# Moving the end of one row of x to the end of the queue, with new cuts of the last loads

## The chip, the cores and the metric

One core of one Trainium2 chip. The metric is the device time of one execution in microseconds; a program on one core has one such time per execution. All runs quoted here are of the fast state and had a granted clock of 1.0.

## The reference

```python
batch, dim = 1024, 4096            # x and y: float32, random normal
def reference(x, y, axis):          # axis = -1
    return np.sum((x - y) ** 2, axis=axis).astype(np.float32)
```

Each of the 128 partitions gets 8 rows of 4096 columns, so 32,768 columns of x and as many of y. "Columns" below are columns per partition: 128 columns of one input are 128 x 128 x 4 bytes, 65.5 KB.

## The kernel before

All loads are issued from one engine (SyncE) and so form one queue. Lists of widths say how x and y are cut. VectorE subtracts (into x's buffer), ACT squares and sums; the last piece alone is squared and summed by VectorE, in one fused instruction that starts from ACT's partial sum of row 3. The parts that the argument touches:

```python
xw = [4096, 12288, 8192, 5472, 1280, 960, 320, 160]
yw = [16256, 8192, 2624, 2784, 1344, 480, 480, 288]
late, last = 128, 192
LATE = 3
halved = (1, 2, 3, 4)                 # loads of y whose pieces are cut in two
cut = (LATE + 1) * D - late           # the last 128 columns of row 3 ...
# [...] xs is xw in order; ys is yw in order without those 128 columns, and then
ys += [(N - last, N), (cut, cut + late)]   # ... come last of all of y
# [...]
    order = []                        # an x load goes ahead of the first y load that needs it
    have = 0
    for c0, c1 in ys:
        while have < c1:
            order.append((landed_x, xv, X, "x") + xs[len([o for o in order if o[3] == "x"])])
            have = order[-1][5]
        order.append((landed_y, yv, Y, "y", c0, c1))
# [...]
    for j, (c0, c1) in enumerate(ys):
        final = j == len(ys) - 1
        wait_loaded(c1, landed_y[j][1])           # VectorE waits for y and the x it needs
        for piece in pieces_of(j, c0, c1):
            sub(*piece)                           # VectorE: x - y
            if final:                             # VectorE: square, sum, add ACT's sum
                nc.vector.wait_ge(diffs, n["diffs"])
                nc.vector.tensor_tensor_reduce(...)
                continue
            square(*piece, where[piece])          # ACT: square with a sum
# [...]
        if j == 4:
            for r in (4, 5, 6):
                complete(r)           # VectorE adds the parts of a row
    complete(7)                       # waits for ACT's last sum
    nc.sync.wait_ge(sums, n["sums"])
    nc.sync.dma_start(out=ov, in_=results).then_inc(stored, 16)
```

## Time and profile before

| | before |
|---|---|
| time, median of the first 3 runs | 83.98 us (83.97 to 84.12) |
| span of the profiled execution | 82.6 us |
| DMA engines, share of the span | 95.9% |
| VectorE, ACT | 45%, 40% |
| last load landed / last reduction starts / store issued | 80.25 / 80.99 / 81.18 us |

The prediction below shows the page's lines, the waits, the chain of waits and the end of the timeline. One reading of the trace recurs here: the landing records. A load's semaphore is incremented 16 times, once for each DMA engine that carries a part of it, and a wait for the load is satisfied at the sixteenth. This is as the Trainium skill has it ("DMA: Bandwidth & Descriptors", section "Why a DMA increments its semaphore by 16 and not by 1"); the trace has 16 records for each of the 18 loads and for the store. In the kernel before, the sixteen increments of a load lay 0.21 to 0.26 us apart from first to last. "Landed" is the last of them, "mean landing" the mean of the sixteen.

### The profile page before, as it was taken

How to read it: one execution, taken by the hardware profiler on the slowest of the kernel's cores; microseconds unless marked ns; L12 is line 12 of the kernel's file. 1: busy time of each engine (PE TensorE's matmuls, PEld its weight loads, DVE VectorE, ACT ScalarE, POOL GpSimd, SP SyncE). 2: the span in 40 equal slices, each digit the busy share in tenths (PEclk: the TensorE clock that was granted, in tenths of full speed). 3: DMA queues.
4: the chain of work that ended last, by engine and by line, in shares of the span. 5: the costliest groups of instructions: out<-in, count | busy, mean ns of one | idle time of the engine just before them, and what ended most of it. 6: DMA issues, size and time to landing. Idle time of an engine off the chain costs nothing.

```text
span 82.6 us, 136 instructions
## 1 busy us (share of the span) xinstructions
DVE 36.8 (45%) x27; ACT 33.4 (40%) x41; POOL 0.2 (0%) x4
## 2 busy tenths in 40 slices
DVE  0000000000000000000299999999189996989992
ACT  3300000000000000000000979889896999899991
POOL 0000000000000000000000000000000000000000
DMA  5998998888999991999599699969979799999960
GB/s 127 389 500 381 595 547 381 381 381 381 504 504 504 504 504 63 441 504 504 254 508 508 286 476 508 476 286 508 423 339 509 339 437 440 426 402 416 395 220 2
DMA packets 2736, 33.56 MB, mean 406 GB/s; under 512 B 432, under 2 KB 1328, under 8 KB 1712
## 3 DMA queue, kind: packets, MB, share of 16 engines
q1 hardware_dynamic: 2736, 33.56, 95.9%
HBM read 33.55 MB, written 0.00 MB: 406 GB/s over the span
## 4 chain that ended last, share of the span: by engine, by line
DMA 63%; SPq 16%; DVE 12%; ACT 4%; issue 1%
DMA Y<-in_y_dram 63%; SPq L108 16%; DVE X L175 11%; ACT X L181 4%; DVE Y L204 0%; DVE results L188 0%; SPq L220 0%; DVE results L204 0%
## 5 line engine op out<-in xcount | busy, mean ns | idle before, releaser
L175 DVE TENSOR_TENSOR X<-X,Y 128x2048 f32<-128x2048 f32 (+10 forms) x21 | 36.2, 1780 | 44.3 <-DMA Y<-in_y_dram 44.3
L181 ACT ACTIVATE X<-X 128x2048 f32<-128x2048 f32 (+9 forms) x20 | 31.2, 1559 | 46.1 <-DVE X L175 46.0
L181 ACT ACTIVATION_READ_ACCUMULATOR X<-X 128x1 f32 x20 | 3.7, 186 | 0.0
L181 ACT ACT_TABLE_LOAD x1 | 1.3, 1283 | 1.4 <-PEq L19 1.4
L188 DVE TENSOR_REDUCE results<-parts 128x1 f32<-128x2 f32 (+2 forms) x4 | 0.4, 152 | 0.0
L204 DVE CUSTOM_DVE_ANT_0 Y<-X,parts 128x128 f32<-128x128 f32 x1 | 0.4, 352 | 0.0
L250 POOL MEMSET const-bfloat16-1.0<- 128x1 bf16 x1 | 0.1, 101 | 0.0
L250 POOL MEMSET const-uint8-127<- 128x1 uint8 x1 | 0.1, 101 | 0.0
L250 POOL MEMSET const-float32-0.0<- 128x1 f32 x1 | 0.1, 98 | 0.2 <-issue 0.2
L250 POOL MEMSET const-float32-1.0<- 128x1 f32 x1 | 0.1, 98 | 0.0
L204 DVE DVE_READ_ACCUMULATOR2_ANT results<- 128x1 f32 x1 | 0.1, 83 | 0.0
## 6 DMA issues: line engine op xcount, KB each, us to landing
Y<-in_y_dram SPq DMA_DIRECT2D x1, 8128.0 KB, 39.0
X<-in_x_dram SPq DMA_DIRECT2D x1, 6144.0 KB, 20.2
X<-in_x_dram SPq DMA_DIRECT2D x1, 4096.0 KB, 48.3
Y<-in_y_dram SPq DMA_DIRECT2D x1, 4096.0 KB, 57.5
X<-in_x_dram SPq DMA_DIRECT2D x1, 2736.0 KB, 13.3
X<-in_x_dram SPq DMA_DIRECT2D x1, 2048.0 KB, 7.1
Y<-in_y_dram SPq DMA_DIRECT2D x1, 1392.0 KB, 19.0
Y<-in_y_dram SPq DMA_DIRECT2D x1, 1312.0 KB, 16.1
```

The source lines that it names most:

```text
L108: nc.sync.dma_start(out=dst[:, home(c0, c1)], in_=src[:, c0:c1]).then_inc(sem, 16)
L175: nc.vector.tensor_sub(out=a, in0=a, in1=Y[:, home(c0, c1)]).then_inc(diffs, 1)
L181: nc.scalar.activation(out=a, in_=a, func=Square, accum_out=acc).then_inc(acts, 1)
L188: nc.vector.tensor_reduce(out=results[:, r : r + 1], in_=parts_of(r, len(row_parts[r])), axis=mybir.AxisListType.X, op=add,).then_inc(sums, 1)
L204: nc.vector.tensor_tensor_reduce(out=Y[:, home(*piece)], in0=X[:, home(*piece)], in1=X[:, home(*piece)], scale=1.0, scalar=parts_of(r, 1), ...
L250: nc = _bacc.Bacc("TRN2", target_bir_lowering=False, num_devices=1)
```

## The change

The intent: the last 128 columns of row 3 come last of x as well as of y. They add a small load between the last columns of row 7 and the last load of y, so that ACT's last sum and VectorE's fused sum are ready together; the other cuts are fitted to this. The core of the diff (what is left out, the code that waits for the late load of x among it, is marked `[...]`):

```diff
-    xw = [4096, 12288, 8192, 5472, 1280, 960, 320, 160]
-    yw = [16256, 8192, 2624, 2784, 1344, 480, 480, 288]
-    late, last = 128, 192
+    xw = [4096, 12160, 8192, 6784, 736, 384, 288]
+    yw = [16256, 8192, 1344, 1376, 1376, 1376, 1280, 768, 384, 288]
+    late = 128
-    halved = (1, 2, 3, 4)
+    halved = (1, 2, 3, 4, 5, 6, 7)
[...]
-    ys += [(N - last, N), (cut, cut + late)]
[...]
+        return spans + [(cut, cut + late)]
+
+    xs, ys = pieces(xw), pieces(yw)
[...]
-        if j == 4:
+        if j == 6:
             for r in (4, 5, 6):
                 complete(r)
```

The queue ends with (x and y with their columns) x320, y288, x160, y192, y128 before, and x384, y384, x288, y288, x128, y128 after.

More of the change, by code (lines that the diff above doesn't have):

```diff
@@ L68, with pieces @@
     results = nc.alloc_sbuf_tensor("results", [P, R], F32).ap()
-    xw = [4096, 12288, 8192, 5472, 1280, 960, 320, 160]
-    yw = [16256, 8192, 2624, 2784, 1344, 480, 480, 288]
-    late, last = 128, 192
+    xw = [4096, 12160, 8192, 6784, 736, 384, 288]
+    yw = [16256, 8192, 1344, 1376, 1376, 1376, 1280, 768, 384, 288]
+    late = 128
     LATE = 3
-    halved = (1, 2, 3, 4)
+    halved = (1, 2, 3, 4, 5, 6, 7)
     cut = (LATE + 1) * D - late
-    assert sum(xw) == N and sum(yw) == N - late - last
-    xs, c = [], 0
-    for w in xw:
-        xs.append((c, c + w))
-        c += w
-    ys, c = [], 0
-    for w in yw:
-        ys.append((c, c + w))
-        c += w
-        if c == cut:
-            c += late
-    ys += [(N - last, N), (cut, cut + late)]
+    def pieces(widths):
+        spans, c = [], 0
+        for w in widths:
+            spans.append((c, c + w))
+            c += w
+            if c == cut:
+                c += late
+        assert c == N
+        return spans + [(cut, cut + late)]
+    xs, ys = pieces(xw), pieces(yw)
     prog = Program(nc, tc)
@@ L111 @@
     order = []
-    have = 0
-    for c0, c1 in ys:
-        while have < c1:
-            order.append((landed_x, xv, X, "x") + xs[len([o for o in order if o[3] == "x"])])
-            have = order[-1][5]
-        order.append((landed_y, yv, Y, "y", c0, c1))
+    xk = 0
+    for piece in ys:
+        while xk < len(xs) and (xs[xk][0] < piece[1] if xk < len(xs) - 1 else piece == ys[-1]):
+            order.append((landed_x, xv, X, "x") + xs[xk])
+            xk += 1
+        order.append((landed_y, yv, Y, "y") + piece)
     todo = list(order)
@@ L161, with wait_loaded @@
     seen_x = [0]
-    def wait_loaded(c1, ysem):
+    def wait_loaded(c1, ysem, final):
         waits = []
-        while seen_x[0] < len(xs) and xs[seen_x[0]][0] < c1:
+        while seen_x[0] < len(xs) - 1 and xs[seen_x[0]][0] < c1:
             waits.append(seen_x[0])
             seen_x[0] += 1
+        if final:
+            assert seen_x[0] == len(xs) - 1
+            waits.append(seen_x[0])
         nc.vector.wait_ge(ysem, 16)
@@ L197 @@
         final = j == len(ys) - 1
-        wait_loaded(c1, landed_y[j][1])
+        wait_loaded(c1, landed_y[j][1], final)
         for piece in pieces_of(j, c0, c1):
```

## The prediction

> **What bounds the kernel now.** I read the page first: the span, the engines' busy time and the DMA queue.
>
> ```profile
> span 82.6 us, 136 instructions
> ...
> DVE 36.8 (45%) x27; ACT 33.4 (40%) x41; POOL 0.2 (0%) x4
> ...
> q1 hardware_dynamic: 2736, 33.56, 95.9%
> ...
> DMA 63%; SPq 16%; DVE 12%; ACT 4%; issue 1%
> ```
>
> Both compute engines work less than half of the span; the DMA engines work 95.9% of it, which is 79.2 us of 82.6. They carry 33.56 MB, which is exactly both inputs, and the change carries the same bytes. So whatever the change does, it can touch only what is left: the small cost of each load, and what comes after the last byte. Next I read who waited for whom.
>
> ```profile
> DVE X L175 <- DMA Y<-in_y_dram: 44.3, 5, 40.9
> ```
>
> VectorE waited five times, always for a load of y. The first wait (40.9 us, for the 8 MB load) isn't a loss, since loads run under it. What counts is the end, so I read the timeline of the last three microseconds; columns are start, duration, engine, line, operation.
>
> ```profile
> 79.38 0.19 ACT L181 ACTIVATION_READ_ACCUMULATOR X<-X 128x1 f32 x1
> 79.47 0.59 ACT L181 ACTIVATE X<-X 128x480 f32<-128x480 f32 x1
> 79.58 1.06 DVE L175 TENSOR_TENSOR X<-X,Y 128x288 f32<-128x288 f32 x3 [0.15 <-DMA Y<-in_y_dram]
> 79.97 0.19 ACT L181 ACTIVATION_READ_ACCUMULATOR X<-X 128x1 f32 x1
> 80.08 0.44 ACT L181 ACTIVATE X<-X 128x288 f32<-128x288 f32 x1
> 80.42 0.19 ACT L181 ACTIVATION_READ_ACCUMULATOR X<-X 128x1 f32 x1
> 80.52 0.35 ACT L181 ACTIVATE X<-X 128x192 f32<-128x192 f32 x1
> 80.67 0.35 DVE L204 CUSTOM_DVE_ANT_0 Y<-X,parts 128x128 f32<-128x128 f32 x1
> 80.77 0.19 ACT L181 ACTIVATION_READ_ACCUMULATOR X<-X 128x1 f32 x1
> 80.95 0.08 DVE L204 DVE_READ_ACCUMULATOR2_ANT results<- 128x1 f32 x1
> 80.99 0.16 DVE L188 TENSOR_REDUCE results<-parts 128x1 f32<-128x8 f32 x1
> 81.18 0.35 SPq L232 DMA_DIRECT2D out_dram<-results  x1
> ```
>
> The row at 79.58 merges three subtractions: 288, 192 and 128 columns. The last reduction, at 80.99, needs two things: ACT's sum of the 192 columns, read out by 80.96, and VectorE's own fused sum, whose read-out starts at 80.95. So the two arrive together already. After it comes the store: issued at 81.18, landed 1.4 us later at 82.6.
>
> Which load holds this end? The chain of waits stops at this piece:
>
> ```profile
> 66.94 13.12 DMA Y<-in_y_dram
> 80.05 0.02 issue
> 80.08 0.57 DVE X L175 x2
> 80.65 0.03 issue
> 80.67 0.35 DVE Y L204
> ```
>
> So the end is held by the 192-column load of y, landed at 80.05, and not by the last one: the trace's landing records put the 128 columns at 80.25, when VectorE is still in the 192-column subtraction (80.08 to 80.43). The last load is hidden by about 0.1 us.
>
> The same landing records give the price of a load. Landings, with the step from the one before: x5472 66.76; y2624 69.92 (3.16); y2784 73.25 (3.33); x1280 74.78 (1.53); y1344 76.38 (1.60); x960 77.54 (1.16); y480 78.15 and 78.75 (0.60 each); x320 79.15 (0.40); y288 79.56 (0.41); x160 79.79 (0.23); y192 80.05 (0.26); y128 80.25 (0.20). The 8192-column y took 9.72 us for 4.19 MB, 432 GB/s. At that rate 128 columns (65.5 KB) are 0.15 us and took 0.20; 480 (246 KB) are 0.57 and took 0.60. One load more therefore costs 0.03 to 0.05 us; I use 0.035.
>
> **What the Trainium skill says.** "ScalarE: Activation LUTs", section "What ACT_TABLE_LOAD costs": an ACTIVATE with immediate scale and bias takes 186 ns plus 0.833 ns per element, and back-to-back ones overlap by some 93 ns. For 288 columns that is 426 ns; the trace has 443, and a step of 0.44 between starts, because the accumulator read-out follows each one. The trace agrees.
> "VectorE: DVE Perf Modes", "Specifications" and "Walkthrough": 0.96 GHz, and fp32 tensor-tensor work has one result per cycle. That is 1.04 ns per column; the trace's 128x4096 (4421 ns) and 128x128 (285 ns) give 1.042 and a fixed 0.15. It agrees.
> "DMA: Bandwidth & Descriptors", "Bandwidth", measures a 64 KB transfer at 0.95 us and calls everything under 64 KB dominated by descriptors (another issue path than this kernel's). This trace doesn't show such a price for a 64 KB load in a full queue: 0.20 us. The measurement decides.
>
> **The change part by part.**
> 1. Loads: 18 become 19. The end of row 3 of x (128 columns) leaves the second load of x and comes next to last. Cost: one load, +0.035 us on the last landing, so 80.25 becomes about 80.29. This lies on the path.
> 2. The second x load is 65.5 KB less, so y16256 lands at 40.69 in place of 40.84 and the next two groups 0.15 us earlier. All of it is off the path: VectorE catches up with the loads again at 69.95 in any case.
> 3. y2624 and y2784 become 1344 and three of 1376. VectorE needs 2 x (672 to 704 x 1.042 ns + about 0.07) = 1.57 us per 1376 columns; the load takes 1.63 + 0.035 = 1.67. ACT needs 2 x (688 x 0.833 ns + 0.19) = 1.53. Both keep up; nothing gained, as both keep up today.
> 4. The last 192-column piece goes. Pieces of row 7 end 768 (two of 384), 384, 288. VectorE's subtractions rise from 21 to 23 and ACT's squares from 20 to 22, two fixed costs of about 0.07 and 0.1 us each per engine, beside loads.
>
> The end, by counting back 0.20 us per 128 columns and 0.37 for 288 from 80.29: x128 80.09, y288 79.89, x288 79.51, y384 79.14, x384 78.65, y768 78.16.
> - VectorE: 384 at 79.16, free by 79.63; 288 at 79.91 to 80.36, next start possible at 80.28; the last 128 at 80.31 to 80.60, just after its landing; fused sum at 80.63 (80.67 now).
> - ACT: 384 columns cost 0.52 per step. Pieces ready at 78.78, 79.25 and 79.75; it is free again by about 80.32. The 288 are ready at 80.40: 0.34 to the read-out, 0.19 for it, done at 80.93 (80.96 now).
> - Reduction at about 80.94 (80.99 now), store issued at 81.13, landed at 82.55.
> Sum: +0.04 for the load, -0.09 for no longer queueing a 192-column subtraction ahead of the last one: **-0.05 us**. From 83.98 that makes 83.93; the ACT side gives -0.03 and VectorE's -0.04, the same within what I can read, and I put down 83.92.
>
> **The rivals.**
> - *The extra small loads cost more than their bytes.* If the page's price for 64 KB held in this queue, the 128-column x would cost up to 0.75 us more: 84.7. Against it: the 128- and 192-column loads of y are there already and took 0.20 and 0.26.
> - *ACT becomes the last.* Its last piece grows from 192 to 288 columns (347 to 443 ns). If ACT is behind by one piece of 384, its end moves from 80.93 to about 81.1: 84.05. For it: at the end now ACT runs piece on piece with no idle. Against: 384-column pieces arrive every 0.47 to 0.5 us and cost 0.52, so only about 0.1 us piles up before the gap ahead of the 288.
> - *The queue runs dry.* The issuing engine stands still for up to 5.57 us at its last issue, so the ring holds some ten loads. With 19 loads the last issue is later still; if smaller loads filled the ring with less work, transfers could stop. Then it would be 84.5 or more. Against: the last issue now ends at 73.0, 7 us ahead of its landing; ten of the new loads hold as much.
> - *A larger gain.* If the old end were held by the 192-column subtraction alone and the extra load were free, it would be the 0.09 plus the 0.035: 83.86. Nothing shows more: after the last byte the subtraction, fused sum, reduction and store all stay.
>
> **Range and chances.** The three runs of before spread over 0.15 us, and the page's terms can each be off by 0.05. The gain and this spread are alike in size, so 83.70 to 84.15 should hold it 8 times in 10. Two per cent is 1.68 us; the rivals make at most +0.7, and to gain 1.68 the DMA engines would have to carry the same bytes faster. Faster by over 2%: 0.01; within 2%: 0.98; slower: 0.01.
>
> **What would show each step right or wrong.** In the changed kernel's landing records: the last y at 80.25 to 80.35 (step 1), with 0.15 to 0.25 us for each 128-column load. In the chain of waits: the last piece must be the 128-column y load and not the one before it. In the timeline: the fused sum at about 80.63, ACT's last read-out ending at about 80.93, the reduction at 80.94. In the waits: more waits of VectorE for loads of y (every group), in about the same total less 0.15. The prediction would be wrong if the last landing moved by more than 0.1 us, if DMA showed slices with idle engines between 60 and 80 us, or if ACT's last read-out ended after 81.05.

## The result, and the profile after

| | before | changed |
|---|---|---|
| median, 6 runs each | 84.06 us (83.97 to 84.12) | 84.12 us (84.08 to 84.43) |
| ratio of fast runs | | 1.0016, 95% interval 0.9999 to 1.0033 |
| loads | 18 | 19 |
| span of the profiled execution | 82.6 us | 82.8 us |

A ratio is the mean time of the one kernel's fast runs over that of the other's of the same rounds, so it is not quite the ratio of the medians: the means are 84.19 and 84.05 us. The class "same" is right. The predicted gain of 0.05 us is not there. The mean of 84.19 lies above the predicted range, which ended at 84.15; the median of 84.12 lies just inside it. All outputs are right.

The page of the changed kernel, lines that answer to those shown of before (engines with busy time, share and instructions; the DMA queue with packets, MB and share; the chain by engine):

```profile
span 82.8 us, 143 instructions
...
DVE 37.1 (45%) x29; ACT 33.9 (41%) x45; POOL 0.2 (0%) x4
...
q1 hardware_dynamic: 2880, 33.56, 96.0%
...
DMA 58%; SPq 22%; DVE 12%; ACT 4%; issue 1%
```

144 packets more (2736 before): the 128 rows of the new load and its 16 semaphore packets. The bytes are the same. The end of the timeline of the changed kernel (start, duration, engine, line, operation):

```profile
79.90 0.51 ACT L185 ACTIVATE X<-X 128x384 f32<-128x384 f32 x1
80.05 0.72 DVE L179 TENSOR_TENSOR X<-X,Y 128x288 f32<-128x288 f32 x2 [0.28 <-DMA Y<-in_y_dram]
80.31 0.18 ACT L185 ACTIVATION_READ_ACCUMULATOR X<-X 128x1 f32 x1
80.54 0.44 ACT L185 ACTIVATE X<-X 128x288 f32<-128x288 f32 x1
80.81 0.35 DVE L208 CUSTOM_DVE_ANT_0 Y<-X,parts 128x128 f32<-128x128 f32 x1
80.89 0.19 ACT L185 ACTIVATION_READ_ACCUMULATOR X<-X 128x1 f32 x1
81.08 0.08 DVE L208 DVE_READ_ACCUMULATOR2_ANT results<- 128x1 f32 x1
81.11 0.16 DVE L192 TENSOR_REDUCE results<-parts 128x1 f32<-128x8 f32 x1
81.30 0.35 SPq L236 DMA_DIRECT2D out_dram<-results  x1
```

and of its chain of waits (start, duration, what):

```profile
71.49 8.96 DMA Y<-in_y_dram
80.46 0.02 issue
80.48 0.30 DVE X L179
80.78 0.03 issue
80.81 0.35 DVE Y L208
```

The form of the end is the predicted one. The chain now ends in the last load itself, VectorE is free when it lands, ACT's read-out (80.89 + 0.19) and VectorE's (from 81.08) arrive together. Read to the nanosecond, the last reduction starts 32 ns after ACT's read-out ends and 28 ns after VectorE's begins; in the kernel before it was 31 and 38. In two of the experiments (before_xlate, xlate_in_2) ACT was done 0.16 and 0.09 us ahead, and the reduction started in the same nanosecond as VectorE's read-out. So in both kernels it is ACT's sum that comes last, by a hair. But all of it stands 0.15 to 0.18 us later than predicted, because the last load landed at 80.456 and not at 80.29. The landing records divide the 0.205 us between the last landings of the two profiles:

| from before to changed, mean landings | us |
|---|---|
| first load (x4096), whose size did not change: 7.015 to 7.060 | +0.045 |
| 128 columns fewer ahead of the 8192 columns of y | -0.15 |
| from that y (60.164, now 60.058) to the last y (80.145, now 80.292): 19.98 to 20.23 | +0.25 |
| slowest engine behind the mean at the last load: 0.106 to 0.164 | +0.06 |
| sum | +0.205 |

The second row takes back 0.15 of the third, for the 128 columns only changed their place. What is left of the third is +0.10 us, in place of the predicted +0.035 for one load. The first and the last row are a matter of the single execution, if they do not come again. The experiments test this.

### The profile page after: what moved, and what is told of

Same layout as the page of the kernel before. It is cut to its first block, busy times and chain, and to the rows that moved or that the text cites. A ratio compares the mean times of both kernels' runs of the same rounds, so it can differ in the third digit from the quotient of the medians.

```text
span 82.8 us, 143 instructions
## 1 busy us (share of the span) xinstructions
DVE 37.1 (45%) x29; ACT 33.9 (41%) x45; POOL 0.2 (0%) x4
## 4 chain that ended last, share of the span: by engine, by line
DMA 58%; SPq 22%; DVE 12%; ACT 4%; issue 1%
DMA Y<-in_y_dram 58%; SPq L109 22%; DVE X L179 11%; ACT X L185 4%; DVE Y L208 0%; DVE results L192 0%; SPq L224 0%; DVE results L208 0%
## 5 line engine op out<-in xcount | busy, mean ns | idle before, releaser
L179 DVE TENSOR_TENSOR X<-X,Y 128x672 f32<-128x672 f32 (+8 forms) x23 | 36.5, 1638 | 44.1 <-DMA Y<-in_y_dram 44.0
L185 ACT ACTIVATE X<-X 128x672 f32<-128x672 f32 (+7 forms) x22 | 31.5, 1434 | 45.7 <-DVE X L179 45.7
```

The lines of the kernel that those rows point to most:

```text
L179: nc.vector.tensor_sub(out=a, in0=a, in1=Y[:, home(c0, c1)]).then_inc(diffs, 1)
L185: nc.scalar.activation(out=a, in_=a, func=Square, accum_out=acc).then_inc(acts, 1)
```

## The experiments

All measures of loads are from the landing records of one profile per run. "Interval" is the time from the mean landing of the 8192-column y to the mean landing of the last y. "Overhead" is the interval less the bytes at 436 GB/s (a packet of 512 bytes takes 27 ns and one of 65,024 bytes 2400 ns, which makes 27.2 bytes per ns between them; times 16 engines 435, so each overhead is 0.04 us too large, the same in all runs, and no difference hangs on it). "Behind big x" is the same sum for the loads after the 5472 (or 6784) columns of x alone. "Slow packets" is the time by which packets of that big x exceeded the median of their size, divided by 16 engines. It matters, because some executions have such packets and others don't. "Offset" is from the last landing to the start of the last reduction.

| run | loads | interval | overhead | behind big x | slow packets | offset | mean time |
|---|---|---|---|---|---|---|---|
| before | 18 | 19.98 | 0.59 | 0.53 | 0 | 0.74 | 84.05 |
| before_again | 18 | 19.97 | 0.58 | 0.53 | 0 | 0.74 | 84.20 |
| pair_before | 18 | 19.99 | 0.60 | 0.55 | 0 | 0.74 | 84.12 |
| after | 19 | 20.23 | 0.69 | 0.60 | 0.03 | 0.66 | 84.19 |
| after_again | 19 | 20.22 | 0.68 | 0.59 | 0.01 | 0.64 | 84.25 |
| pair_after | 19 | 20.31 | 0.77 | 0.57 | 0.15 | 0.75 | 84.17 |
| x_whole | 18 | 19.97 | 0.58 | 0.49 | 0.01 | 0.91 | 84.27 |
| x_whole_again | 18 | 20.17 | 0.78 | 0.60 | 0.12 | 0.90 | 84.39 |
| before_xlate | 19 | 20.51 | 0.97 | 0.76 | 0.18 | 0.63 | 84.14 |
| x288_in_2 | 20 | 20.32 | 0.78 | 0.68 | 0.03 | 0.70 | 84.25 |
| xlate_in_2 | 20 | 20.60 | 1.06 | 0.81 | 0.19 | 0.63 | 84.37 |
| xlate_early | 19 | 20.36 | 0.82 | 0.57 | 0.17 | 0.89 | 84.62 |
| x5472_in_4 | 21 | 20.19 | 0.80 | 0.52 | 0.05 | 0.74 | 84.29 |
| tail_128 | 18 | 20.02 | 0.63 | 0.57 | 0.02 | 0.80 | 84.23 |

(xlate_early has its moved load behind the big x, so it is counted there. The row "before" gives the mean of the 6 runs of the first comparison. Behind the big x alone the changed kernel has only 0.04 to 0.07 us more than the kernel before, for the cuts differ there; the 6784 columns themselves have 0.03 to 0.05 us more overhead than the 5472. x_whole has the cuts of the changed kernel in both places, so I compare with it.)

### The two kernels again: after_again and before_again

Theory: the loads of the change cost 0.2 us on the last landing. Rival: the profiled execution was late by chance. No edit.

> The changed kernel once more, for its spread. Theory A (the loads of the change really cost 0.2 us on the last landing, where the prediction said 0.035): the last y lands at 80.40 to 80.50 again and the time is 0.10 to 0.20 us above the kernel before. Rival N (the profiled execution was a late one by chance): the last y lands near 80.30 and the ratio to the kernel before is below 1.0005.

> The kernel before under a new label, for the spread of its landings and of its times against itself. Theory A: the last y lands at 80.20 to 80.30 again, ratio within 0.0007 of 1. Rival N: the last landing moves by 0.1 us or more between two profiles of the same kernel.

Measured: the last y landed at 80.37 in the changed kernel and at 80.34 in the kernel before (80.46 and 80.25 in their first profiles). So the absolute landing moves by 0.09 us between two profiles of one kernel, and in this pair the two kernels lie only 0.02 us apart: a good part of the 0.205 us was such chance, and both sides were part right. The interval hardly moves: 20.23 and 20.22, against 19.98 and 19.97. The difference of 0.25 us, of which 0.10 is not bytes, is the kernel's own. From here on I read the interval. Expected and missed: the kernel before under a new label was 1.0021 of itself (0.9998 to 1.0043), as slow as the changed kernel under its own (1.0023, 1.0001 to 1.0045). Times alone can't tell 0.05 us here.

### Without the late load of x: x_whole and x_whole_again

```diff
-    xw = [4096, 12160, 8192, 6784, 736, 384, 288]
+    xw = [4096, 12288, 8192, 6784, 736, 384, 288]
[...]
-    xs, ys = pieces(xw), pieces(yw)
+    xs, ys = pieces(xw, 0), pieces(yw, late)     # the late piece for y alone
[...]
```

> The changed kernel without the late load of x: 7 loads of x and 11 of y, cuts of y and of the rest of x as in the changed kernel. Theory A1 (the extra small load costs most of the 0.2 us): the last y lands at 80.25 to 80.32, the reduction starts near 80.95, time 0.13 to 0.2 us below the changed kernel. Rival A2 (the new cuts of y and x cost it, the extra load only 0.035): the last y lands at 80.40 or later, time within 0.05 us of the changed kernel.

The landing went as the first theory had it: last y at 80.31, interval 19.97, just that of the kernel before. The new cuts of y therefore cost the queue nothing, and the extra load costs 0.25 us less 0.15 for its bytes, 0.10. The time did not fall: 84.27, within 0.05 us of the changed kernel's 84.25, as A2 had it, though the landing shows that A2's reason was wrong. The end of its timeline shows why:

```profile
80.16 0.66 DVE L176 TENSOR_TENSOR X<-X,Y 128x288 f32<-128x288 f32 x2 [0.20 <-DMA Y<-in_y_dram]
...
80.65 0.44 ACT L182 ACTIVATE X<-X 128x288 f32<-128x288 f32 x1
80.85 0.35 DVE L205 CUSTOM_DVE_ANT_0 Y<-X,parts 128x128 f32<-128x128 f32 x1
81.00 0.19 ACT L182 ACTIVATION_READ_ACCUMULATOR X<-X 128x1 f32 x1
81.13 0.08 DVE L205 DVE_READ_ACCUMULATOR2_ANT results<- 128x1 f32 x1
81.22 0.16 DVE L189 TENSOR_REDUCE results<-parts 128x1 f32<-128x8 f32 x1
```

The last y is now only 0.18 us behind the 288 columns. VectorE is still in their subtraction, and ACT's sum of them (read out by 81.00 + 0.19) comes after VectorE's read-out begins (81.13): the reduction waits for ACT, 0.91 us after the last landing in place of 0.66. With a piece of 288 columns ahead, the late load of x pays: the 0.2 us that it takes in the queue is time in which this piece is finished.

> The changed kernel without its late load of x, once more, for a second profile of its landings. The overhead of the loads after the 6784 columns of x (sum of each load's step between mean landings less its bytes at 436 GB/s) was 0.49 us there and 0.595 and 0.593 in two profiles of the changed kernel. Theory T (0.10 us for the late load of x): 0.48 to 0.51 again. Rival N (chance): 0.55 or more.

This repeat missed: overhead 0.60 behind the big x, 0.78 in all. It is an execution with slow packets: the 27,136-byte packets of the 6784 columns took 0.12 us too long on average over the engines, the 32,768-byte ones 0.13 and the 5376-byte ones 0.05. Its offset, 0.90, agrees with the first. Set beside pair_after, the profile of the changed kernel with slow packets (0.57 behind the big x), it would give the late load no cost at all; profiles with slow packets can't measure 0.1 us. For the landing, the verdict thus rests on one clean profile of x_whole, and I wanted the cost of a load from another side.

### One load more among the small ones, of the same size: x288_in_2

```diff
-    xw = [4096, 12160, 8192, 6784, 736, 384, 288]
+    xw = [4096, 12160, 8192, 6784, 736, 384, 160, 128]
```

> The changed kernel with its 288-column load of x as two loads, 160 and 128 columns: one load more, no bytes more, none under 512 bytes a row. Same sum of overheads, 0.595 in the changed kernel. Theory T (each load of some 128 columns among the small ones costs 0.10): 0.68 to 0.71. Theory P (packets alone, 0.075): 0.67. Prediction's figure (0.035): 0.63. If the sum grows by 0.18 or more, as in the cut into two loads of 64, the floor of 0.2 us a load begins above 128 columns.

Overhead behind the big x 0.68 against 0.59 and 0.60: +0.08 to 0.09 for one load, in a profile with hardly any slow packets. No byte was added, and nothing else moved. The interval agrees: 20.32 against 20.22. The prediction's 0.035 (0.63) is out; 0.10 and the packets' 0.075 are both near.

### One load more of 64 columns: xlate_in_2

```diff
+    xs[-1:] = [(cut, cut + 64), (cut + 64, cut + late)]
[...]
```

> The changed kernel with its late 128 columns of x as two loads of 64: one load more, no bytes more, among the small ones at the end. The same interval was 20.23 and 20.22 us in two profiles of the changed kernel. Theory T (a small load in the tail costs 0.10 us): 20.32. Prediction's 0.035: 20.26. The reduction starts later by the same amount, 0.04 or 0.10 after that of the changed kernel at an equal landing of the 8192-column y.

Behind the big x +0.22, twice what was expected, and the times go the same way (ratio 1.0030, 1.0012 to 1.0048). The steps between mean landings tell why: the two loads of 64 columns took 0.204 and 0.198 us, the last load of 128 columns 0.188. Half the bytes took no less time. The engines' packets got shorter (18 ns for 256 bytes, 27 ns for 512), eight of them and the 9 ns semaphore packet make 0.15 us, but the loads came in 0.20. Something other than the packets sets the pace there; what it is, no record shows. (The profile had slow packets too, but in the 6784 columns, ahead of this sum.)

### Loads more, far from the end: x5472_in_4

```diff
-    xw = [4096, 12288, 8192, 5472, 1280, 960, 320, 160]
+    xw = [4096, 12288, 8192, 1368, 1368, 1368, 1368, 1280, 960, 320, 160]
[...]
```

(Left out is the line that keeps the four together ahead of y2624.)

> The kernel before with its x load of 5472 columns cut into four of 1368: three loads more, no bytes more, far from the end. Measured by the time from the mean landing of the 8192-column y to the mean landing of the last y, which was 19.98 and 19.97 us in two profiles of the kernel before. Theory F (every load has a fixed cost of 0.10 us whatever its place): 20.27. Theory of the prediction (0.035 each): 20.08. Theory P (cost by packets: eight of about 8 ns each per engine and a 9 ns semaphore packet, 0.075 a load): 20.20.

The interval grew by 0.20 to 0.22 us for three loads, 0.07 each, as the packets alone would have it. Some 0.05 us of it are slow packets of these loads, so 0.05 to 0.07 each. By this one profile a load in the bulk is cheaper than the 0.09 to 0.10 among the small ones, but not as cheap as 0.035.

### The late load of x alone, and elsewhere: before_xlate, xlate_early

```diff
-    xw = [4096, 12288, 8192, 5472, 1280, 960, 320, 160]       # in the kernel before
+    xw = [4096, 12160, 8192, 5472, 1280, 960, 320, 160]       # and (cut, cut + late) as the last of x
[...]
```

> The kernel before with nothing but the end of row 3 of x moved next to last, as an eighteenth-of-nineteen load of 128 columns. Theory A1: the last y lands 0.15 to 0.2 us later than in the kernel before (80.40 to 80.45); as 0.1 of this was hidden there, the time grows by 0.05 to 0.12 us. Rival A2: the last y lands at 80.28 to 80.31 and the time is the same within 0.03 us.

For the cost of a load this run is inconclusive: the interval grew by 0.53 us, of which 0.15 are bytes and 0.24 slow packets (0.18 in x5472, 0.04 in y2624, 0.02 in y2784), and the profiled execution was the slowest of its six (84.33; the others 84.01 to 84.21). For the other half of the change it is the cleanest test, for nothing moved but this load:

```profile
80.75 0.36 ACT L187 ACTIVATE X<-X 128x192 f32<-128x192 f32 x1
81.02 0.19 ACT L187 ACTIVATION_READ_ACCUMULATOR X<-X 128x1 f32 x1
81.09 0.35 DVE L210 CUSTOM_DVE_ANT_0 Y<-X,parts 128x128 f32<-128x128 f32 x1
81.37 0.08 DVE L210 DVE_READ_ACCUMULATOR2_ANT results<- 128x1 f32 x1
81.37 0.16 DVE L194 TENSOR_REDUCE results<-parts 128x1 f32<-128x8 f32 x1
```

The last y landed at 80.74, the reduction starts at 81.37: offset 0.63, against 0.74 in all three profiles of the kernel before. So the gap that the late x opens ahead of the last subtraction is worth 0.11 us: VectorE starts that subtraction at once, and ACT is done in time. Its ratio, 1.0010 (0.9994 to 1.0025), agrees with a load that pays back what it costs, but would not show 0.05 us.

```diff
+    xs.insert(4, xs.pop())          # in the changed kernel: the late x right behind the 6784 columns
[...]
```

> The changed kernel with its late 128 columns of x loaded right after the 6784 columns of x and not next to last; as many loads and bytes. Theory T (the cost is that of a small load among small ones): the interval falls from 20.22 to 20.15 or less. Theory F (a load costs the same anywhere): 20.20 to 20.23. In both, the last y now lands 0.2 us behind the 288 columns and not 0.4, so ACT's square of the 288 becomes the last: reduction 0.88 to 0.92 us after the last landing (0.64 to 0.66 in the changed kernel), time 0.1 to 0.25 us above the changed kernel.

The cost by place stays open: the interval was 20.36 with 0.17 us of slow packets in the 6784 columns alone. Less these it is 20.19, nearer to theory F's 20.20 than to theory T's 20.15, but one such profile settles nothing. What both theories expected of the end came: offset 0.89, ACT last, and a time above that of the changed kernel, by more than I had said (84.62 against 84.25 in after_again, ratio 1.0060 to the kernel before). Of the two places tried, the load is worth its cost only next to last.

### Shorter last piece without a further load: tail_128

```diff
-    xw = [4096, 12288, 8192, 5472, 1280, 960, 320, 160]
-    yw = [16256, 8192, 2624, 2784, 1344, 480, 480, 288]
-    late, last = 128, 192
+    xw = [4096, 12288, 8192, 5536, 1280, 960, 320, 96]
+    yw = [16256, 8192, 2688, 2784, 1344, 480, 480, 288]
+    late, last = 128, 128
```

> The kernel before with its last but one piece cut from 192 to 128 columns (64 columns go to the first of the cuts): 18 loads as before. If the 192-column piece held the end by 0.09 us, as the prediction said, then without a load more the end comes earlier: the reduction starts 0.66 to 0.70 us after the last landing (0.74 and 0.75 in the two profiles of before), time 0.03 to 0.08 us below before. Rival: ACT, which works piece on piece there, is the last and takes it all: 0.73 or more, time the same.

The rival held: offset 0.80, and the time is not better (ratio 1.0014, 1.0001 to 1.0026). ACT worked piece on piece up to its last read-out at 80.99 to 81.18, later than VectorE's read-out (from 81.06): the shorter piece helps VectorE, and ACT is the one that comes last. In this profile the engines were also further apart from the start (16 increments of the last load over 0.50 us), so the offset itself is one execution's. As an attempt to beat both kernels it failed.

### Both kernels a third time, treated alike: pair_after and pair_before

> The changed kernel a third time, beside the kernel before under a new label of its own, so that both are treated alike (the kernel before against itself gave 1.0021 under a new label). Theory: the dearer load (0.09 to 0.10 us) and the gap that it opens ahead of the last subtraction (0.09 to 0.11 us) cancel, so its mean is within 0.10 us of that of the other label. The overhead of the 13 loads after the 6784 columns is 0.59 to 0.60 us where no bulk packets were slow; the reduction starts 0.63 to 0.66 us after the last landing. The prediction's own sum (0.035 a load) would have it 0.05 us below.

> The kernel before a third time, under a new label. Overhead of the 12 loads after the 5472 columns 0.52 to 0.54 us, reduction 0.73 to 0.75 us after the last landing. Ratio to the runs of the kernel before between 1.000 and 1.003, which shows what a new label alone does.

Measured on the same chip beside each other: 84.17 and 84.12 us, ratios 1.0006 (0.9991 to 1.0021) and 1.0007 (0.9994 to 1.0021). Any difference is within the noise, and the predicted 0.05 us is too small for these times to rule out. The profile of pair_before is like the other two. That of pair_after was of its slowest execution (84.34): slow packets of 0.15 us, and its engines 0.68 us apart at the last load, so that the 288 columns landed only 0.34 us ahead of it in place of 0.43 and 0.45. ACT was last and the offset 0.75, which I had not expected.

## Why the prediction was wrong, step by step

- **What bounds the kernel**: right. The DMA queue is 96% busy in both, and the end follows the last landings.
- **One load more on the path, +0.035 us**: wrong in size; this is the step that failed. In the profiles with hardly any slow packets a load more cost 0.10 us (x_whole to changed) and 0.09 (x288_in_2). The prediction took the step between two landings, subtracted the bytes, and called the rest the price of a load. The new load's own step is 0.203 us, 0.05 over its bytes, as that reckoning has it; the rest of the 0.10 falls on its neighbours: the 288-column y ahead of it takes 0.40 to 0.41 us in the three profiles of the changed kernel and 0.37 and 0.38 in those of x_whole. Why the neighbours pay is open. (The rate that it used, 432 GB/s, has some fixed cost in it already, but at 436 the bytes of 128 columns still are 0.15 us; that was not the cause.)
- **No subtraction queued ahead of the last one, -0.09 us**: right. The offset fell from 0.74 to 0.66 and 0.64 (not in pair_after, 0.75, where the loads landed too close); by the late x alone (before_xlate) to 0.63.
- **Sum, -0.05 us**: with the measured terms it is +0.10 and -0.08 to -0.11, thus about zero; the times of pair_after and pair_before agree with that, within their noise.
- **x lands earlier, off the path; new cuts of y cost nothing and gain nothing**: right. x_whole has the interval of the kernel before. More waits of VectorE were predicted, one for every group; the view lists four, and five before, for VectorE reached the groups of 1376 columns just as they landed (before_again lists four as well).
- **The rivals**: the first, that small loads cost more than their bytes, named the right place. Its size, up to 0.75 us, came from the page; I set it aside with the 0.20 of a step, which was right against 0.75 and too much trust in 0.05. ACT did come last, in all but two of the 14 profiles, but in five of the six of these two kernels by no more than 0.04 us; it was 0.07 to 0.15 in x288_in_2 and where the last loads landed too close (both of x_whole, xlate_early, pair_after, tail_128), and 0.02 in x5472_in_4. In the changed kernel's first profile ACT's read-out ended at 81.08, past the 81.05 that the prediction gave as a sign of being wrong, because all had moved with the last landing. The queue did not run dry: the last issue of the changed kernel began at 71.49, 9 us ahead of its landing. The larger gain has a slip in its sum: with a free load the 0.09 alone is left, 83.89, and not 0.09 plus 0.035.
- **The range**: three runs within 0.15 us were taken for the spread. The 17 fast runs of the changed kernel under three labels reach from 83.97 to 84.59, the kernel before under a new label to 84.62. Its upper end, 84.15, left no room for that tail. The base was low as well: 83.98 was the median of three runs, and the means of the kernel before were 84.05, 84.12 and 84.20 later. Of the 0.27 us between the predicted 83.92 and the mean of 84.19, the load's price makes 0.06 to 0.07; the rest is this base (0.07 to 0.22, by the mean that one takes) and the scatter of the runs.

Open: why some executions have slow packets in the 5472 or 6784 columns of x. Among profiles with the 6784 columns, four of eight exceeded 0.1 us, and these four also had their engines 0.53 to 0.68 us apart at the last load (0.30 to 0.40 in the other four); of those with the load of 5472 (or 5536) columns one of five did. Too few to blame the longer load. Open too is whether the 0.2 us per small load is a matter of the loads themselves or of their being queued behind one another.

## What to carry to other kernels

A further small load at the end of a full queue cost more here (0.10 us) than the difference between its landing step and its bytes (0.05): measure such a price by adding one with no bytes more and comparing an interval inside the trace, not by its own step. It can still pay as a spacer, if an engine needs that time to finish the piece ahead of it; here the two cancel. With differences near 0.1% a kernel must be compared with the old one under a label of its own, and read from landings within the trace rather than from total times.

## What the Trainium skill lacked or had wrong

- "DMA: Bandwidth & Descriptors", section "Bandwidth": it gives 0.95 us for a 64 KB transfer (another issue path). No figure is given for what a further small load costs in a full queue. Here a 64 KB load took a step of 0.18 to 0.21 us, a 32 KB load 0.20, and a further load cost 0.09 to 0.10 us among small ones and, by one profile, 0.05 to 0.07 in the bulk, bytes not counted.
- The same page, section "Specifications", has 512 bytes as the least transfer for line rate. Packets of 512 bytes took 27 ns here, 19.0 bytes per ns, against 27.1 in packets of 65,024 bytes (2400 ns): 70% of it.
- The same page, section "Why a DMA increments its semaphore by 16 and not by 1", says that the engines finish independently, and the trace agrees; it has no figure for how far apart. Here the last load's increments were 0.21 to 0.68 us apart, different in each execution of the same kernel, and the wait lasts until the slowest.
- No page that I read mentions executions in which bulk packets run slow: 0.12 to 0.19 us per engine over one load of 21,888- to 27,136-byte packets, in five of the profiles.
